# An MLP's first product moved to sevens with early-staged sums, and every engine in source order

## The chip, the cores and the metric

One core of a Trainium2 chip runs the kernel. The metric is the device time of one execution, in microseconds (us). TensorE (PE) multiplies, VectorE (DVE), ScalarE (ACT) and GpSimd (POOL) do the rest, and SyncE (SP) issues the transfers.

## The reference

A hybrid decoder layer on 1024 tokens of width 1024: a gated merge of dilated attention and an RWKV-7 recurrence, then a squared-ReLU MLP, then a gated embedding. The change lies in the MLP alone:

```python
f = rmsnorm(h, ffn_pre_norm[i])
f = jnp.square(jax.nn.relu(f @ w_ff_in[i])) @ w_ff_out[i]      # 1024 -> 4096 -> 1024
h = h + rmsnorm(f, ffn_post_norm[i])
```

## The kernel before

The kernel is written as generators that yield the time of each TensorE step. A planner (`Order`) walks them on a model clock: dense work in `sch.add`, chains of other work in `sch.spawn`. So the order of TensorE's instructions is the order in which the planner emits them (`manual_schedule` for PE holds throughout). SP keeps the order of the source in most of the MLP too. VectorE, ScalarE and GpSimd are placed by the compiler's scheduler between the end of the recurrence and the last part of the MLP; elsewhere `manual_schedule(engines=OTHERS)` puts them in source order as well.

Each float32 product is three matmuls (`mm3`): both operands are split into a high half (a ScalarE copy to fp32r) and a low half (a subtraction on VectorE or GpSimd), and high x high, high x low and low x high are accumulated in PSUM.

**First matrix.** Its 32 column blocks of 128 (`ff1`) are multiplied plainly: each block for two token halves of 512, over eight chunks of 128 of the width, 24 matmuls of 128x512 each time. `wload` fetches a block (`wr`) and splits it into `wh` and `wl`; `ff1_evac` applies ReLU and squares into `raw_h`. The normalised activations `f` come from `mixed(i)`, one chain for each of eight token tiles, whose end `put_T` transposes them (`tp`) and splits them. `ff1_first` starts on token half 0 while the tiles of half 1 are still made.

**Second matrix.** Two column blocks of the first matrix make a pair, which is 256 rows of the second. Fifteen of the sixteen pairs are multiplied in seven block products in place of eight (Winograd's form of Strassen): the pair's activations make four blocks (two of 128 rows x two token halves), and the weights four (two of 128 rows x two halves of 512 columns). `operands` builds the sums on GpSimd (`sum`, `ws`), `split2` splits them (`duo`), and `product` runs 4 x 3 matmuls per block product and adds each result from PSUM to `tot` on VectorE. `prep(n + 2)` is called at the start of product n. The seven products stand between the half blocks of the next pair's first matrix. The last pair is multiplied plainly in `ff2_last`.

**Beside it.** `part` splits the weights of the last stage once and stores both halves in DRAM (`gp`, `gpl`, `pkg`), one unit every three products. `e_weights` and `last_weights` load them for the stage after the MLP.

```python
MUL = (2, 1, 6, 5, 3, 7, 4)
INTO = {1: (0, 0), 6: (1, 0), 5: (1, 1), 3: (0, 1), 7: (1, 1), 4: (1, 0), 2: (0, 0)}
FIRST = (2, 1, 7)                     # products that open a new PSUM bank; the others add to the last one
```

Of the kernel before, what the change touches and what calls it, by code (L numbers as in the profile page):

```python
# [10 lines left out]
F32 = mybir.dt.float32  # L11
# [233 lines left out]
def layer(ctx: ExitStack, tc: tile.TileContext, x, pT, wz, wup, w_out, wff1, w_ff2, w_ple, w_pleg,  # L245
# [1067 lines left out]
    class Split:  # L1313
        def __init__(self, pcs):
            self.p = [k2(t) for t in pcs]

        def __getitem__(self, key):
            _, k, t = key
            return self.p[k // 2][:, k % 2, t]

# [43 lines left out]
    def out_1(i):  # L1364
        def body():
            h, ts = tok(i)
            if i == 0:
# [4 lines left out]
                pc = pieces(GA, "f0", F32R)  # L1372
                fT[0][0], fT[1][0] = Split(pc[0:4]), Split(pc[4:8])
# [7 lines left out]
    fT = [[None, None], [None, None]]  # L1381
# [9 lines left out]
    def put_T(srcs, hi, lo, i):  # L1391
        ts = slice(i * 128, i * 128 + 128)
        for b in range(2):
# [3 lines left out]
            if isinstance(hi, Split):  # L1397
                for q in range(2):
                    o = 2 * b + q
                    S.activation(hi.p[o][:, :, ts], ps[:, 2 * q:2 * q + 2, :], AF.Copy)  # L1400
                    V.tensor_tensor(lo.p[o][:, :, ts], ps[:, 2 * q:2 * q + 2, :], hi.p[o][:, :, ts],
                                    OP.subtract)
            else:
                o = (slice(None), slice(4 * b, 4 * b + 4), ts)
                S.activation(hi[o], ps, AF.Copy)
                V.tensor_tensor(lo[o], ps, hi[o], OP.subtract)
            sch.hold(tag)

    def mixed(i, ps):
        h = i // 4  # L1410
        yield from wait(lambda: i == 0 or ("M", i - 1) in done and (i < 2 or i - 2 in t_f))
        if i == 4:
            for p in range(2):
                fT[p][1] = mtile("hl"[p], 0, [128, KT, 512], f"f1{p}", F32R)
# [15 lines left out]
        yield from put_T(hh, fT[0][h], fT[1][h], i % 4)  # L1430
        t_f[i] = sch.dep + 0.1

# [10 lines left out]
    def totals():  # L1443
        for m in range(2):
            tot.append(mtile("hl"[m], 1, [128, 2, 4, 512], f"tot{m}", F32))

    def acc(i, c):
        return tot[i // 4][:, c, i % 4]

    def ff1_half(ps, hi, lo, h):  # L1450
        return mm3(ps, [(hi[:, k * 128:(k + 1) * 128], lo[:, k * 128:(k + 1) * 128],
                         fT[0][h][:, k, slice(0, 512)], fT[1][h][:, k, slice(0, 512)]) for k in range(KT)])

    def ff1_evac(ps, j, h):
        p, x = j // 2, 2 * (j % 2) + h
        if p not in raw_h:
            raw_h[p] = rtile([128, 4, 512], "hr", ("BK", "UV")[p % 2])
# [72 lines left out]
    def prep(n):  # L1530
        p, i = n // 7, MUL[n % 7]
        if p >= NP - 1:
            return
# [403 lines left out]
```

## Time and profile before

| what | value |
|---|---|
| time, median of 3 runs | 1776.96 us (1774.38 to 1780.42) |
| profiled execution: time, span | 1773.19 us, 1771.4 us |
| mean granted TensorE clock | 0.999 |
| busy share PE / DVE / ACT / POOL | 98% / 57% / 41% / 38% |
| MLP, first to last matmul of the fifteen pairs | 982.4 to 1626.1 us |
| DMA over the span | 175.51 MB, mean 99 GB/s |

The span runs from the first to the last instruction; the time has some 2 us more around it. A busy share counts pipelined matmuls by their length, so 98% says that TensorE hardly ever had nothing in flight, not that each matmul was at its best pace. In the tables of groups a line reads: source line, engine, operation, output and inputs, shapes, count, then busy time, mean ns of one, and the idle time ahead of it with what ended it.

### The profile page before, as it was taken

To read this page: it belongs to the slowest core of one execution; us is meant where nothing else is said; L and a number is where in the kernel's file an instruction comes from. 1 tells how busy PE (TensorE), PEld (TensorE's weight loads), DVE (VectorE), ACT (ScalarE), POOL (GpSimd) and SP (SyncE) were. 2 spreads that over 40 slices of the span, in tenths; PEclk is the share of its full clock that TensorE was granted. 3 is DMA by queue.
4 is the path that set the end of the run, shared out by engine and by line. 5 is a ranking of instruction groups with operands and counts; after the bars stand their busy time and mean duration, and the time that the engine had idled before them with its cause. 6 is when DMAs were issued, how large, how long until landed. Compare 5 with 4: busy or idle time off the path is not lost.

```text
span 1771.4 us, 25935 instructions
## 1 busy us (share of the span) xinstructions
PE 1743.8 (98%) x10192; PEld 1423.4 (80%) x10192; DVE 1017.1 (57%) x1834; ACT 732.3 (41%) x1315; POOL 670.5 (38%) x423
## 2 busy tenths in 40 slices
PE   9999989999999999999999999999999999999998
PEld 8787877878877777778888878888788888888887
DVE  6289777776534233353735466665666566556643
ACT  5824343432344343542434434343334334333454
POOL 1344131231232323332230266666665566652311
PEclk9999999999999999999999999999999999999999
DMA  4621121212332222333524132332232232305611
GB/s 163 211 95 37 49 78 47 98 43 96 86 134 84 60 60 72 110 111 135 201 96 139 64 113 95 94 115 87 92 118 91 84 95 90 123 9 179 214 48 48
DMA packets 67132, 175.51 MB, mean 99 GB/s; under 512 B 7745, under 2 KB 8129, under 8 KB 66498
## 3 DMA queue, kind: packets, MB, share of 16 engines
q1 hardware_dynamic: 67010, 173.86, 29.6%
q8 instruction: 80, 1.31, 0.3%
q14 instruction: 42, 0.34, 0.1%
HBM read 125.20 MB, written 41.94 MB: 94 GB/s over the span
## 4 chain that ended last, share of the span: by engine, by line
PE 82%; DVE 5%; DMA 5%; ACT 3%; POOL 2%; issue 2%; SPq 0%; DVEq 0%; ACTq 0%; POOLq 0%
PE z L294 18%; PE z L296 18%; PE z L292 18%; PE bk L292 6%; PE bk L294 5%; PE bk L296 5%; PE sc L275 1%; DVE xy L113 1%; PE y L275 1%; PE po L275 1%; PE pt L283 1%; PE A L275 1%; PE wr L275 1%; PE fq L275 1%; POOL wl L113 1%
## 5 line engine op out<-in xcount | busy, mean ns | idle before, releaser
L113 POOL TENSOR_TENSOR wl<-wr,wh 128x1024 fp32r<-128x1024 f32 (+1 forms) x87 | 208.0, 2392 | 431.4 <-ACT wh L113 412.2
L113 DVE TENSOR_TENSOR tot<-tot,bk 128x512 f32<-128x512 f32 x420 | 272.7, 682 | 129.9 <-PE bk L296 129.7
L292 PE MATMUL z<-uh,wh 128*128 128x512 f32 (+1 forms) x800 | 312.3, 390 | 5.5 <-ACT part L113 3.0
L296 PE MATMUL z<-uh,wl 128*128 128x512 f32 (+1 forms) x800 | 312.6, 391 | 2.7 <-POOL wl L113 2.7
L294 PE MATMUL z<-ul,wh 128*128 128x512 f32 (+1 forms) x800 | 313.6, 392 | 1.3 <-DVE ul L113 1.3
L292 PE MATMUL z<-f,wh 128*128 128x512 f32 x496 | 193.2, 389 | 0.3 <-ACT f L113 0.3
L294 PE MATMUL z<-f,wh 128*128 128x512 f32 x496 | 193.1, 389 | 0.2 <-DVE f L113 0.2
L296 PE MATMUL z<-f,wl 128*128 128x512 f32 x496 | 193.0, 389 | 0.0
L292 PEld LDWEIGHTS z<-uh,wh 128*128 128x128 f32 x800 | 151.1, 189 | 36.2 <-ACT part L113 3.5
L296 PEld LDWEIGHTS z<-uh,wl 128*128 128x128 f32 x800 | 151.0, 189 | 34.1 <-POOL wl L113 4.0
L294 PEld LDWEIGHTS z<-ul,wh 128*128 128x128 f32 x800 | 151.2, 189 | 32.3 <-issue 3.6
L292 PE MATMUL bk<-duo 128*128 128x512 f32 x420 | 164.3, 391 | 4.0 <-DVE tot L113 3.9
L294 PE MATMUL bk<-duo 128*128 128x512 f32 x420 | 163.5, 389 | 0.0
L296 PE MATMUL bk<-duo 128*128 128x512 f32 x420 | 163.5, 389 | 0.0
L113 ACT ACTIVATE wh<-wr 128x1024 fp32r<-128x1024 f32 (+1 forms) x87 | 90.3, 1038 | 119.0 <-PE z L294 89.8
L113 POOL TENSOR_TENSOR duo<-w2r,duo 128x512 fp32r<-128x512 f32 x45 | 66.7, 1483 | 166.0 <-ACT duo L113 166.0
L113 POOL TENSOR_TENSOR duo<-ws,duo 128x512 fp32r<-128x512 f32 x60 | 81.0, 1350 | 122.3 <-ACT duo L113 119.0
L292 PEld LDWEIGHTS z<-f,wh 128*128 128x128 f32 x496 | 93.1, 188 | 20.0 <-ACT f L113 0.5
L294 PEld LDWEIGHTS z<-f,wh 128*128 128x128 f32 x496 | 93.1, 188 | 19.8 <-DVE f L113 0.5
L296 PEld LDWEIGHTS z<-f,wl 128*128 128x128 f32 x496 | 93.1, 188 | 19.2
L292 PEld LDWEIGHTS bk<-duo 128*128 128x128 f32 x420 | 78.8, 188 | 23.7 <-DVE tot L113 7.0
L296 PEld LDWEIGHTS bk<-duo 128*128 128x128 f32 x420 | 78.8, 188 | 16.4
(312 smaller groups left out, 3203.5 us busy)
## 6 DMA issues: line engine op xcount, KB each, us to landing
wr<-in_wz_dram SPq DMA_DIRECT2D x48, 512.0 KB, 3.7
wr<-in_wff_dram SPq DMA_DIRECT2D x31, 512.0 KB, 3.6
w2r<-in_w_ff_dram SPq DMA_DIRECT2D x30, 512.0 KB, 4.2
xt<-in_x_dram SPq DMA_DIRECT2D x16, 512.0 KB, 4.3
gscr<-gst SPq DMA_DIRECT2D x32, 256.0 KB, 2.0
g<-gscr SPq DMA_DIRECT2D x16, 512.0 KB, 4.2
wpg<-pkg SPq DMA_DIRECT2D x16, 512.0 KB, 6.7
sw<-qk SPq DMA_DIRECT2D x48, 128.0 KB, 2.3
```

The lines of the kernel that those rows point to most:

```text
L113: return f(*a, **kw)
L275: PE.matmul(out_, a, b, start=start, stop=stop)
L283: PE.transpose(out_, a, ident if idn is None else idn)
L292: PE.matmul(ps, ah, bh, start=start and i == 0, stop=False, skip_group_check=not start)
L294: PE.matmul(ps, ah, bl, start=False, stop=False, skip_group_check=not start)
L296: PE.matmul(ps, al, bh, start=False, stop=i == n - 1, skip_group_check=not start)
```

## The change

The first matrix goes to sevens too. Its blocks are: the activations' two halves of the width (512 each) for two token halves, and for each pair of column blocks four quarters of the weights. `put_f` makes seven operand tiles F[1] to F[7] from the activations once (for token half 1, six more ScalarE copies and the sums and low halves on VectorE and GpSimd, per token tile). Products 1 and 2 of a pair need only token half 0. All 32 of them (`early`) run first, 27 of them before token half 1 is asked for; the first product is stored to DRAM (`p1_scr`), their sum is activated and stored (`c_scr`). `take(p)` loads them back for each pair, `first` runs the other five products (6, 5, 7, 3, 4), and VectorE adds them to the loaded blocks. GpSimd makes the weights' sums (`w1_sum`), each in the place of a quarter, which `w1_raw` reloads.

The second matrix is multiplied in sevens for every other pair (`seven`, pairs 0, 2, ... 14) and plainly for the seven between (`plain`). For the sevens, the sums of weights are made and split one round ahead (`w2_sums`), stored to DRAM (`bs_scr`) and loaded back as operands. `pend` holds low-half subtractions and some transfers back until the next `flush()`, one chunk of three matmuls or one block later. `part` runs in the plain rounds, four units each.

From the first pair's five products on, `manual_schedule(engines=OTHERS)` holds for VectorE, ScalarE, GpSimd and SP.

```diff
-        yield from put_T(hh, fT[0][h], fT[1][h], i % 4)
+        yield from put_f(hh, i)
...
+    def put_f(srcs, i):
...
+        t2, t4 = (rtile([128, 4, 128], n, tag) for n, tag in (("t2", "pg"), ("t4", "yc")))
+        V.tensor_tensor(t2, d, at(1, 0), OP.add)
+        V.tensor_tensor(t2, t2, at(1, 1), OP.add)
+        G.tensor_tensor(c, c, at(1, 0), OP.subtract)
+        G.tensor_tensor(c, c, at(1, 1), OP.subtract)
+        G.tensor_tensor(t4, at(2, 0), t2, OP.subtract)
+        G.tensor_tensor(t4, t4, at(2, 1), OP.add)
+        for n, x, eng in ((7, d, V), (6, t2, V), (5, c, G), (4, t4, G)):
+            S.activation(at(n, 0), x, AF.Copy)
+            eng.tensor_tensor(at(n, 1), x, at(n, 0), OP.subtract)
...
-    MUL = (2, 1, 6, 5, 3, 7, 4)
+    MUL = (1, 6, 5, 3, 7, 4, 2)
-    FIRST = (2, 1, 7)
+    FIRST = (1, 7, 2)
...
+    SEQ = (6, 5, 7, 3, 4)
...
+    def w1_split(j):
...
+        S.activation(w[:, 0], src, AF.Copy)
+        lo = lambda: (V if j < NA and j % 4 == 3 else G).tensor_tensor(w[:, 1], src, w[:, 0], OP.subtract)
+        lo() if j < NA else pend.append(lo)
+
+    def w1_sum(p, n):
...
+        if n == 1:
+            G.tensor_tensor(at("s1"), at(21), at(22), OP.add)
+        if n == 2:
+            G.tensor_tensor(at(21), at(11), at(21), OP.subtract)
+        if n == 3:
+            G.tensor_tensor(at(11), at("s1"), at(11), OP.subtract)
+        if n == 4:
+            G.tensor_tensor(at(12), at(12), at(11), OP.subtract)
...
+    def early(j):
+        k, p, i = prods[j]
+        if k != 25:
+            a_raw(min(k + 6, NE) if k != 26 else 31)
...
+        yield from w1_mm(j, ps, i == 1)
+        dst = A_["out"][:, k % (4 if k < NA else 2)]
+        if i == 1:
+            S.activation(dst, ps, AF.Copy)
+        else:
+            S.activation(dst, ps, AF.Relu)
+            S.activation(dst, dst, AF.Square)
+        SY.dma_start((p1_scr if i == 1 else c_scr)[p], dst)
...
+    def first(j):
+        k, p, i = prods[j]
+        n = SEQ.index(i)
+        if n == 3:
+            if p == 0:
+                w1_sum(1, 1)
+                w1_sum(1, 2)
+            w1_sum(p + 1, 3)
+        if p:
+            w1_split(j + 2)
+        late = p == 0
+        if n == 0 + late:
+            pend.append(lambda: w1_raw(p + 1, 21, 22, 11))
+        if n == 1 + late:
+            pend.append(lambda: w1_raw(p + 1, 12))
+        if n == 2 and p:
+            w1_sum(p + 1, 1)
+            w1_sum(p + 1, 2)
+        if n == 4:
+            w1_sum(p + 1, 4)
...
+        yield from w1_mm(j, ps, n < 2)
+        x = raw_h[p][:, {6: 1, 5: 3, 7: 3, 3: 1, 4: 2}[i]]
+        V.tensor_tensor(x, x, ps, OP.add)
+        if i in (7, 3, 4):
+            S.activation(x, x, AF.Relu)
+            S.activation(x, x, AF.Square)
...
+    def mlp():
+        last["turn"] = tc.manual_schedule(engines={mybir.EngineType.SP})
+        last["turn"].__enter__()
+        while sch.t < t_f.get(3, 1e9):
+            yield 0.0
+        for j in range(NA):
+            beside(j)
+            yield from early(j)
+        while sch.t < t_f.get(7, 1e9):
+            yield 0.0
+        last["turn"].__exit__(None, None, None)
+        last["turn"] = tc.manual_schedule(engines=OTHERS)
+        last["turn"].__enter__()
+        for n in range(5):
+            beside(NA + 2 * n)
+            yield from chunks(4 * n + 4)
+            beside(NA + 2 * n + 1)
+            Y["j"] += 1
+            yield from early(NA + 2 * n + 1)
+            flush()
+        prep(0)
+        prep(1)
+        flush()
+        for p in range(1, NP):
+            Y["n"] = 0
+            e = p - 1
+            if e % 2 == 0:
+                for x in range(7):
+                    yield from chunks((20 * x + 23) // 7 if p < NP - 1 else (3, 6, 9, 13, 17, 20, 20)[x])
+                    yield from seven(items.index((e, x)))
+                    if x == 0:
+                        load_w2(p)
+                    if x == 4:
+                        take(p + 1)
...
+                continue
+            for u in range(8):
+                yield from chunks((20 * u + 23) // 8)
+                if u == 0:
+                    load_w2(p)
+                yield from plain(items.index((e, u // 2)), u % 2)
+                if u == 1:
+                    take(p + 1)
+                    w2_sums(p, 0)
+                if 0 < u < 6:
+                    w2_sums(p, u)
+                part(2 * p - 4 + u // 2, u % 2)
...
     def split2(t, tag, eng):
         d = rtile([128, 2, 512], "duo", tag, F32R)
         S.activation(d[:, 0], t, AF.Copy)
-        eng.tensor_tensor(d[:, 1], t, d[:, 0], OP.subtract)
+        pend.append(lambda: eng.tensor_tensor(d[:, 1], t, d[:, 0], OP.subtract))
         return d
...
     def prep(n):
...
+        if e % 2 == 0:
+            i, room = MUL[x], rooms(e)[x % 3]
+            a = split2(operand(e, i), room[0], G)
+            if i in (2, 1, 3):
+                b = split2(w_blocks(e)[{2: 2, 1: 0, 3: 3}[i]], room[1], G)
+            else:
+                b = rtile([128, 2, 512], "duo", room[1], F32R)
+                SY.dma_start(b.bitcast(F32), bs_scr[e, i])
+            duo[n] = a, b
+            return
...
+    def plain(n, part):
+        e, x = items[n]
+        if part == 0:
+            prep(n + 2)
+        m, c = 1 - x // 2, x % 2
+        a, (hi, lo) = duo[e, m], ops["w"]
+        for t in (2 * part, 2 * part + 1):
+            ts = slice(t * 128, t * 128 + 128)
+            ps = bank(XB)
+            yield from mm3(ps, [(a[j][:, 0, ts], a[j][:, 1, ts], hi[:, j, halves[c]], lo[:, j, halves[c]])
+                                for j in range(2)])
+            V.tensor_tensor(tot[m][c][:, t], tot[m][c][:, t], ps, OP.add)
+            flush()
...
+    def part(u, x):
...
+            gp["t"] = rtile([128, 512], "gp", "gst")
+            SY.dma_start(gp["t"], src[:, c] if len(src.shape) == 2 else src[:, u % 2])
             return
+        raw, hi = gp["t"], rtile([128, 512], "gph", "gst", F32R)
+        lo = raw.bitcast(F32R)
         S.activation(hi, raw, AF.Copy)
         V.tensor_tensor(lo, raw, hi, OP.subtract)
         SY.dma_start(dst[:, k, 0, c], hi.bitcast(F32))
         SY.dma_start(dst[:, k, 1, c], lo.bitcast(F32))
...
-    ff1_first()
-    for j in range(2, 2 * NP):
-        ff1(j)
+    sch.add(mlp)
```

More of the change, by code (lines that the diff above doesn't have):

```diff
@@ L1444, in totals @@
         for m in range(2):
-            tot.append(mtile("hl"[m], 1, [128, 2, 4, 512], f"tot{m}", F32))
+            t = rtile([128, 2, 4, 512], "tot", GA[m])
+            tot.append([t[:, 0], t[:, 1]])
     def acc(i, c):
[L1448 to L1456, printed above, removed]
-            raw_h[p] = rtile([128, 4, 512], "hr", ("BK", "UV")[p % 2])
-        f1 = rtile([128, 512], "f1", "gst")
-        S.activation(f1, ps, AF.Relu)
-        S.activation(raw_h[p][:, x], f1, AF.Square)
-        if x == 3 and p == NP - 1:
-            last_split(1, (1,), ())
+        return tot[i // 4][c][:, i % 4]
@@ new lines, in w1_slot, with w1_raw @@
+    def w1_slot(p, n):
+        if n == 22:
+            return W1[22, p % 2]
+        if n == "s1" and p == 0:
+            if "s10" not in W1:
+                W1["s10"] = rtile([128, 512], "sum", "ex")
+            return W1["s10"]
+        return W1[n]
+    def w1_raw(p, *names):
+        for n in names:
+            if p < NP:
+                SY.dma_start(w1_slot(p, n), quarter(p, (11, 12, 21, 22).index(n)))
+    early_ = []
+    for p in range(0, NP, 2):
+        early_ += [(p, 1), (p + 1, 1), (p, 2), (p + 1, 2)]
@@ new lines, in layer, with chunks, take @@
+    Y = {"j": NA, "g": None, "n": 0}
+    def chunks(n):
+        while Y["n"] < n:
+            if Y["g"] is None:
+                Y["g"] = first(Y["j"])
+                Y["j"] += 1
+            for _ in range(3):
+                yield next(Y["g"])
+            flush()
+            Y["n"] += 1
+            if Y["n"] % 4 == 0:
+                for _ in Y["g"]:
+                    pass
+                Y["g"] = None
+    def take(p):
+        if p < NP:
+            raw_h[p] = rtile([128, 4, 512], "hr", ("BK", "UV")[p % 2])
+            for x, src in ((1, p1_scr), (3, p1_scr), (2, p1_scr), (0, c_scr)):
+                SY.dma_start(raw_h[p][:, x], src[p])
@@ L1464, in last_split, with mlp_ahead @@
+    def mlp_ahead(x):
+        if x == 0:
+            w1_tiles()
+            for k in range(4):
+                a_raw(k)
+        else:
+            for j in range(3):
+                w1_split(j)
+            a_raw(4)
+            a_raw(5)
     def last_split(k, hs, ws):
@@ L1538, in layer, with seven @@
+    XB = ("s1", "s2", "s3", "m0", "m1")
     chain = [None] * 4
-    def product(n):
-        p, i = n // 7, MUL[n % 7]
+    def seven(n):
+        p, x = items[n]
+        i = MUL[x]
         prep(n + 2)
@@ L1683, in last_weights @@
     def last_weights():
-        pg = pieces(GA, "wpg", F32R)
-        P["wpg"] = [[Split(pg[4 * p:4 * p + 4]), mtile("hl"[p], 0, [128, KT, 512], "wpg", F32R)]
-                    for p in range(2)]
+        P["wpg"] = [[mtile("hl"[p], 1 - c, [128, KT, 512], "wpg", F32R) for c in range(2)] for p in range(2)]
         P["g3"] = rtile([128, D], "g3", "v")
```

300 lines of the change are left out of this document (172 added, 128 removed).

## The prediction

> **What bounds the kernel now.** I read the page first: busy shares, clock, chain. Then I took windows over the MLP, its groups by line, its waits, and two pieces of the timeline.
>
> ```profile
> span 1771.4 us, 25935 instructions
> PE 1743.8 (98%) x10192; PEld 1423.4 (80%) x10192; DVE 1017.1 (57%) x1834; ACT 732.3 (41%) x1315; POOL 670.5 (38%) x423
> PEclk9999999999999999999999999999999999999999
> PE 82%; DVE 5%; DMA 5%; ACT 3%; POOL 2%; issue 2%; SPq 0%; DVEq 0%; ACTq 0%; POOLq 0%
> ```
> TensorE is busy nearly always, at full clock, and holds 82% of the chain. The time is a count of matmuls times a spacing, plus a few stalls. The MLP is z<-f (first matrix) and bk<-duo (second matrix):
>
> ```profile
> L292 PE MATMUL z<-f,wh 128*128 128x512 f32 x496 | 193.2, 389 | 0.3 <-ACT f L113 0.3
> L292 PE MATMUL z<-f,w 128*128 128x512 f32 x16 | 6.3, 395 | 0.0
> L292 PE MATMUL bk<-duo 128*128 128x512 f32 x420 | 164.3, 391 | 4.0 <-DVE tot L113 3.9
> L283 PE MATMUL tp<-cs,hh 128*128 128x128 f32 x24 | 3.1, 272 | 0.0
> ```
> Of z and bk each row stands for three (lines 292, 294, 296): (496 + 16) x 3 = 1536 matmuls for the first matrix and 420 x 3 = 1260 for the second, 2796 together. 389 ns is the pipelined length of one, not its price. The price is the spacing:
>
> ```profile
> 1402.12 0.39 PE L292 MATMUL z<-f,wh 128*128 128x512 f32 x1
> ...
> 1413.00 0.39 PE L292 MATMUL z<-f,wh 128*128 128x512 f32 x1
> ```
> Between these two starts lie four groups of twelve (half a z block, one product, twice): 10.88 / 48 = 0.2267 us each. At that, 2796 are 633.9 us. The windows (columns: PE, PEld, DVE, ACT, POOL busy, clock, DMA share, GB/s):
>
> ```profile
> 982.00:1010.00 28.00, 27.47 (x132) 22.55 (x131) 12.86 (x25) 14.11 (x30) 7.34 (x6) 1.00 0.09 34
> 1010.00:1050.00 40.00, 38.67 (x169) 31.00 (x168) 23.54 (x37) 13.80 (x24) 25.63 (x18) 1.00 0.30 105
> 1080.00:1240.00 160.00, 160.00 (x707) 132.34 (x706) 99.01 (x146) 62.12 (x102) 100.26 (x66) 1.00 0.29 93
> 982.00:1626.00 644.00, 639.49 (x2823) 526.83 (x2822) 389.10 (x579) 248.06 (x412) 381.02 (x253) 1.00 0.28 92
> ```
> The MLP fills 982.4 to 1626.1, 643.7 us. Beyond its 633.9 us lie 24 transposes (tp, under 3.1 us) and stalls of some 7 us: 644.00 - 639.49 = 4.5 us shown as TensorE idle, the rest restarts. In the steady stretch (third row) TensorE never idles, GpSimd is at 63% and VectorE at 62%. What TensorE waits for, and what the others wait for, in the MLP:
>
> ```profile
> PE bk L292 <- DVE tot L113: 3.9, 4, 1.7
> POOL duo L113 <- ACT duo L113: 235.7, 74, 34.4
> DVE tot L113 <- PE bk L296: 142.0, 58, 13.5
> ```
> The helpers wait for TensorE and each other; it hardly waits for them. One exception is worth seeing:
>
> ```profile
> 1241.35 0.63 ACT L113 ACTIVATE gp<-gp 128x512 fp32r<-128x512 f32 x1 [5.16 <-DMA gp<-in_w_pleg_dram]
> 1242.01 0.69 DVE L113 TENSOR_TENSOR gpl<-gp 128x512 fp32r<-128x512 f32 x1 [5.07 <-ACT gp L113]
> 1242.62 0.68 DVE L113 TENSOR_TENSOR tot<-tot,bk 128x512 f32<-128x512 f32 x1
> 1243.35 0.50 PE L292 MATMUL bk<-duo 128*128 128x512 f32 x1 [1.70 <-DVE tot L113]
> ```
> A late load blocked ScalarE, the subtraction behind it blocked VectorE, and the accumulation behind that cost TensorE 1.70 us. That is what an in-order engine does with one late operand.
>
> **The matmuls.** First matrix: a pair of 256 columns took 2 x 2 x 8 x 3 = 96 matmuls; in sevens it takes 7 x 4 x 3 = 84. Sixteen pairs: 1536 becomes 1344. Second matrix: fifteen pairs in sevens (84 each) become eight in sevens and seven plain (96): 1260 becomes 1344. Net -192 + 84 = -108, times 0.2267 = **-24.5 us**. All are 128x512, so the spacing holds. Up to 982 us the matmuls are the same, and behind 1626 us too (only tags move).
>
> **What helpers must do per pair.** From pair 1 on, a round has 60 matmuls of the first matrix (five products; two were staged early) and 84 or 96 of the second: 144 x 0.2267 = 32.6 us and 156 x 0.2267 = 35.4 us, where a round was 180 x 0.2267 = 40.8 us. Prices:
>
> ```profile
> L113 POOL TENSOR_TENSOR duo<-ws,duo 128x512 fp32r<-128x512 f32 x60 | 81.0, 1350 | 122.3 <-ACT duo L113 119.0
> L113 POOL TENSOR_TENSOR duo<-w2r,duo 128x512 fp32r<-128x512 f32 x45 | 66.7, 1483 | 166.0 <-ACT duo L113 166.0
> L113 POOL TENSOR_TENSOR ws<-w2r 128x512 f32<-128x512 f32 x30 | 47.0, 1569 | 11.2 <-PE tp L283 5.5 <-DMA w2r<-in_w_ff_dram 3.0 <-PE bk L296 0.8
> L113 DVE TENSOR_TENSOR tot<-tot,bk 128x512 f32<-128x512 f32 x420 | 272.7, 682 | 129.9 <-PE bk L296 129.7
> L113 DVE TENSOR_TENSOR duo<-hr,duo 128x512 fp32r<-128x512 f32 x45 | 40.6, 901 | 0.4 <-ACT duo L113 0.4
> L113 ACT ACTIVATE hr<-f 128x512 f32<-128x512 f32 x64 | 40.4, 632 | 1.9
> L113 ACT ACTIVATE f<-z 128x512 f32<-128x512 f32 x64 | 37.5, 586 | 35.1 <-PE z L296 35.0
> ```
> GpSimd, round with sevens: 5 low halves and 4 sums for the first matrix, 7 low halves for the second, 4 for the plain pair that follows: 20. Plain round: 5 + 4, 3 for the next sevens, 4 sums and 4 low halves staged to DRAM: 20. At 1.40 (between 1.35 and 1.57, nearer the larger group) that is 28.0 us, 86% and 79%. VectorE: with sevens 28 + 5 accumulations at 0.682 and 4 others at 0.90, 26.1 us (80%); plain 16 + 5 and 8 others, 21.5 us (61%). ScalarE: 24 copies or squares at 0.63 in either, 15 us. All fit under TensorE, so no engine becomes the bound by its work alone.
>
> **Order.** In order, an engine that is 86% full has to be fed in time. A second-matrix operand is prepared at the start of product n for product n + 2: two products of 12 x 0.2267 = 2.72 us and two runs of 20 / 7 chunks (0.68 us, three matmuls) of the first matrix, 9.3 us. GpSimd's largest burst is 4 operations a product (5.6 us against 4.6 us of TensorE), so it falls 1 to 2 us behind and recovers: cost 0, cover 9 us. An accumulation chain is rewritten one product later, 4 us of cover for 0.68 us of VectorE. ScalarE waits once per pair for GpSimd's sum before a weight copy (1.4 us), needed 13 us later. SP's reload of a quarter waits for GpSimd's subtraction of its old content; behind it on SP stands the load of a staged operand, with those 9.3 us of lead.
>
> Staging adds DMA: quarters read again 8.4 MB, first products written 8.4 and read 16.8, second-matrix sums written 16.8 and read 16.8, 67 MB on 59 now (92 GB/s x 644 us). 126 MB in about 620 us are 204 GB/s, a share near 0.6. Landing times:
>
> ```profile
> w2r<-in_w_ff_dram SPq DMA_DIRECT2D x28, 512.0 KB, 4.0
> gp<-in_w_pleg_dram SPq DMA_DIRECT2D x16, 256.0 KB, 2.7
> pkg<-gpl SPq DMA_DIRECT2D x16, 256.0 KB, 4.8
> L132 SPq DMA_DIRECT2D pkg<-gp x16: 326/425/474, 1242.0 to 1507.6; - x16
> wpg<-pkg SPq DMA_DIRECT2D x5, 512.0 KB, 8.1
> ```
> The last row is of the crowded end of the MLP. At 4.0 us a staged load is well inside its 9.3 us; at 8.1 us, with one subtraction of 1.4 us ahead of it on SP, it is 0.2 us late, 6 us over the 32 staged loads. I take 0, as three of the four rows are far under the lead, and keep 6 as the bound.
>
> **Where I expect new stalls.** (a) 982 to 1010: ten early products ask ScalarE for 1.53 us each (a copy 0.63, an evacuation of 0.59 or 0.59 + 0.63, on average 0.90), four token tiles for six copies (14.4 us), two norm chains of three squares and small steps for some 6: 36 us in 28. The tiles aren't needed until product 27, 73 us on, so 0 if products go first, 8 if not; 3 taken, nearer 0, because the first window shows ScalarE half idle and TensorE losing 0.53. (b) First pair: 120 matmuls, 27.2 us, for 19 GpSimd operations, 26.6 us. Then the first second-matrix product stands nine matmuls (2.0 us) behind its preparation: evacuation 1.2, two copies 1.3, two subtractions 2.8, 5.3 us. Bounds 0 and 8; 4 taken, a little over 5.3 - 2.0. (c) The four units of gate-weight staging in each plain round. One buffer makes load, copy, subtraction, store a loop: 2.7 + 0.6 + 0.7 + 4.8 + two issues of 0.4 = 9.6 us, where 35.4 / 4 = 8.8 us stand between one load and the next (three products, 3 x 40.8 / 7 = 17.5 us, before). It slips 0.8 us a unit, 2.4 us by the last, behind which VectorE's accumulations stand as at 1242.01; five banks cover about 4. Bounds 0 and 4 a round; 0.7 taken, 5 in seven rounds. (d) Elsewhere 1 (bounds 0 and 6, by the staged loads). Sum 13, against 7 that go with the old code: +6.
>
> **Sum.** 1773.19 (the profiled execution; span 1771.4) - 24.5 + 6 = 1754.7, a gain of 18.5. That execution is 3.8 us under the median of the runs, 1776.96, so the forecast is **1758 us**, 1.0% faster.
>
> **A rule of the Trainium skill.** The longest against the median duration (min/median/max) tells what slows what:
>
> ```profile
> L113 POOL TENSOR_TENSOR duo<-ws,duo x60: 1279/1295/1807, 1005.0 to 1608.5; 128x512 fp32r<-128x512 f32 x60
> L113 DVE TENSOR_TENSOR tot<-tot,bk x420: 671/681/689, 1023.3 to 1663.5; 128x512 f32<-128x512 f32 x140
> L113 DVE TENSOR_TENSOR duo<-hr,duo x45: 674/692/1712, 992.0 to 1607.9; 128x512 fp32r<-128x512 f32 x45
> ```
> The accumulation, which reads one operand from PSUM, never stretches; subtractions with both operands in SBUF do, by up to 1.0 us, and GpSimd's by 0.5. A round now has 4 to 8 such VectorE operations where it had about 9. The Trainium skill, SBUF — State Buffer, section "SBUF: two separate sides", says that VectorE and GpSimd share a port pair under an exclusive lock, and that a VectorE operation takes it only in a two-port mode or with two SBUF inputs. It would speak against filling both engines to 80%. By that rule and these rows, GpSimd would need 20 x 1.29 + 4 x 0.69 = 28.6 us with sevens and 31.3 us plain: still under TensorE, the sum unchanged. The trace agrees.
>
> **Rivals.** (1) Given back in waits: every round loses 1.6 us in waits of the kind at 1241.35 to 1243.35, 15 x 1.6 = 24, while some 5 of the old 7 go: 1777 - 24.5 + 24 - 5, about **1772**. For it: four engines in strict order and twice the DMA. Against: a lead of 9.3 us where that stall had none. (2) Slower: GpSimd keeps waiting for ScalarE's copies. It waited 235.7 us in the MLP, 15.7 a pair; if w us a round stay, a round lasts 28.0 + w, and the loss is 8 (28.0 + w - 32.6) + 7 (28.0 + w - 35.4) = 15 w - 88.6. From w = 7.5 it eats the whole 24.5; at w = 8.5, about half of today's, 39 is lost: 1776.96 - 24.5 + 39 - 7 = **1784**. For it: ScalarE itself now stands in order behind late evacuations. Against: most of those 235.7 us are idleness for want of work, and subtractions are issued a chunk behind their copies. (3) No new stalls, and the old 7 us gone: 1777 - 24.5 - 5 = **1747**. (4) The change doesn't do what it says: fewer than 108 matmuls saved; the source excludes that.
>
> **Chances.** Forecast with gains of 10 to 24 us (1753 to 1767): 0.60. No stalls: 0.08. Given back: 0.16, of which 0.10 within 0.3% (5.3 us, about what a measurement tells from no change) and 0.06 faster. GpSimd-bound: 0.16. So faster 0.74, same 0.10, slower 0.16. The range, 1745 to 1785, takes in the no-stall case and rival 2 at its price; what lies beyond is some 0.05 below and 0.10 above. The upper ends of (a) to (d) together, 8 + 8 + 28 + 6 - 7 - 24.5 = +18.5, would reach 1795, which I leave out as four ends at once.
>
> **What would show it.** In the trace after: 2688 matmuls of 0.2267 spacing in an MLP of about 625 us; GpSimd near 82% in the rounds; TensorE idle near the first early products, behind the first pair and late in plain rounds, each by a few us. GpSimd idle under 4 us a round refutes rival 2, TensorE idle over 20 us in the MLP refutes the sum, and a bs load landing after its product's start would show the DMA bound that I priced at nothing.

## The result, and the profile after

| what | before | after |
|---|---|---|
| time, median of the runs | 1777.09 us (1774.38 to 1780.42) | 1840.64 us (1836.35 to 1844.69) |
| profiled execution: time, span | 1773.19 us, 1771.4 us | 1837.83 us, 1836.0 us |
| mean granted TensorE clock | 0.999 | 0.983 |
| data moved | 175.51 MB | 242.66 MB |

The changed kernel is slower: a ratio of 1.0356, with a 95% interval of 1.0323 to 1.039. The forecast was 1758 us, 0.989 of the time before. On the page of the kernel after, the matmuls are indeed fewer (10084, which is 10192 - 108), but TensorE's share of the chain of waits has fallen from 82% to 63%:

```profile
span 1836.0 us, 26373 instructions
...
PE 1753.1 (95%) x10084; PEld 1417.0 (77%) x10084; DVE 1051.2 (57%) x1799; ACT 751.6 (41%) x1377; POOL 776.8 (42%) x532
...
PE 63%; DVE 10%; DMA 8%; POOL 8%; ACT 5%; issue 4%; SPq 1%; POOLq 0%; DVEq 0%; ACTq 0%
```

Two windows of the same kernel, one over the early products and one over the MLP (columns as in the prediction: PE, PEld, DVE, ACT, POOL busy, clock, DMA share, GB/s):

```profile
990.00:1060.00 70.00, 54.40 (x217) 42.16 (x216) 39.26 (x40) 36.43 (x73) 53.18 (x36) 0.90 0.38 128
...
990.00:1690.00 700.00, 643.51 (x2714) 516.33 (x2712) 418.19 (x549) 272.11 (x486) 492.22 (x363) 0.97 0.51 181
```

TensorE, which lost 0.53 us in the first 28 us of this stage before, is idle for 70.00 - 54.40 = 15.6 us in the first window, and for 700.00 - 643.51 = 56.5 us in all of the second. The granted clock, 1.00 in every window of before, is 0.90 and 0.97.

The waits of the changed kernel over the MLP (total, times, longest). The first row is VectorE's, the others are TensorE's five largest:

```profile
DVE gp L113 <- ACT gph L113: 92.3, 25, 8.3
...
PE bk L292 <- DMA duo<-bs: 16.9, 7, 3.6
PE bk L292 <- DVE tot L113: 15.9, 8, 2.6
PE bk L292 <- ACT pa L113: 15.6, 7, 5.5
PE z L296 <- POOL wl L113: 1.8, 1, 1.8
PE bk L294 <- POOL duo L113: 1.6, 1, 1.6
```

Three causes of much the same size. The timeline has one case of each (start, length, engine, operation, idle time ahead and its releaser):

```profile
997.64 0.63 ACT L113 ACTIVATE f<-t 128x512 fp32r<-128x512 f32 x1 [2.75 <-POOL t L113]
...
1000.43 0.59 ACT L113 ACTIVATE pa<-bk 128x512 f32<-128x512 f32 x1
...
1001.07 0.79 PE L292 MATMUL bk<-f,wl 128*128 128x512 f32 x1 [5.48 <-ACT pa L113]
...
1001.66 0.63 PE L294 MATMUL bk<-f,wl 128*128 128x512 f32 x1
...
1002.65 1.72 POOL L113 TENSOR_TENSOR wh<-wa,wh 128x512 fp32r<-128x512 f32 x1
...
1003.16 1.76 DVE L113 TENSOR_TENSOR t<-d,f 128x512 f32<-128x512 f32 x1
...
1004.34 1.72 POOL L113 TENSOR_TENSOR c<-c,f 128x512 f32<-128x512 f32 x1
...
1004.85 1.76 DVE L113 TENSOR_TENSOR f<-d,f 128x512 fp32r<-128x512 f32 x1
...
1006.09 0.63 ACT L113 ACTIVATE f<-c 128x512 fp32r<-128x512 f32 x1 [3.03 <-POOL c L113]
...
1187.27 0.63 ACT L113 ACTIVATE wl<-wr 128x512 fp32r<-128x512 f32 x1 [2.85 <-POOL wr L113]
...
1188.33 0.62 ACT L113 ACTIVATE gph<-gp 128x512 fp32r<-128x512 f32 x1
...
1188.98 1.32 DVE L113 TENSOR_TENSOR gp<-gp,gph 128x512 fp32r<-128x512 f32 x1 [5.06 <-ACT gph L113]
...
1193.29 1.66 DVE L113 TENSOR_TENSOR sum<-sum,hr 128x512 f32<-128x512 f32 x1
...
1194.87 1.27 DVE L113 TENSOR_TENSOR tot<-tot,bk 128x512 f32<-128x512 f32 x2
...
1195.60 0.50 PE L292 MATMUL bk<-duo 128*128 128x512 f32 x1 [1.35 <-DVE tot L113]
...
1421.81 0.33 SPq L132 DMA_DIRECT2D gp<-in_w_pleg_dram  x1
...
1422.50 0.50 PE L292 MATMUL bk<-duo 128*128 128x512 f32 x1 [2.30 <-DVE tot L113]
...
1425.99 0.32 SPq L132 DMA_DIRECT2D pkg<-gph  x1
...
1426.57 1.29 POOL L113 TENSOR_TENSOR wh<-wr,wh 128x512 fp32r<-128x512 f32 x1 [2.63 <-ACT wh L113]
...
1426.72 0.32 SPq L132 DMA_DIRECT2D pkg<-gp  x1
...
1427.88 1.28 SPq L132 DMA_DIRECT2D wr<-in_wff_dram  x3
...
1429.21 0.43 SPq L132 DMA_DIRECT2D duo<-bs  x1
...
1432.96 0.39 PE L296 MATMUL z<-f,wh 128*128 128x512 f32 x1
...
1435.64 0.47 PE L292 MATMUL bk<-duo 128*128 128x512 f32 x1 [2.29 <-DMA duo<-bs]
```

First stretch, the early products. GpSimd and VectorE take turns: 1002.65, 1004.34 on the one, 1003.16, 1004.85 on the other, each 1.7 us long, where VectorE's subtraction took 0.69 (median) in the kernel before. ScalarE stands in its queue at copies whose sums GpSimd has not made (2.75 us at 997.64, 3.03 at 1006.09), and the evacuation of a bank (`pa`, 1000.43) stands behind them: for that TensorE waited 5.48 us. Once started, a matmul lasts 0.63 us in place of 0.39.

Second stretch, a plain round. ScalarE waits for GpSimd's `wr`, so the copy `gph` of the staged gate weights is late; VectorE stands 5.06 us at its subtraction, does two slow sums, and reaches the accumulation (`tot`) at 1194.87. TensorE waited 1.35 us for it.

Third stretch, the start of a round with sevens. The first product starts at 1422.50, and the staged operand for 1433.2 should be asked for there. SyncE issues it at 1429.21, because two things stand ahead of it. The two stores of the last staging unit (`pkg`) wait for ScalarE's copy and VectorE's subtraction of weights whose load was issued only at 1421.81; they go out at 1425.99 and 1426.72. Behind them the reload of three quarters (`wr`, 1427.88) waits for GpSimd's subtraction, which ended at 1426.57 + 1.29 = 1427.86, and its three issues take another 1.28 us. The staged load then takes 6.3 us to land, behind the reload's transfers. The last matmul before the operand starts at 1432.96, and the next one 2.68 us later. The two stores stand there in six of the seven rounds in which TensorE waited for a staged operand.

To sum such losses up, I took the distance between the starts of neighbouring 128x512 matmuls from 930 us on, less 0.2267 us each. An excess of more than 0.28 us in one distance is "gap"; smaller ones are "half pace" (the short restart behind every wait is among them).

| from 930 us on | gap | half pace | largest gaps by what they waited for |
|---|---|---|---|
| before | 5.5 us | 3.0 us | tot 5.0 |
| after | 65.1 us | 25.4 us | staged operand 18.0, tot 17.7, pa 16.7 |

The account closes: -24.5 (108 matmuls) + 59.6 (gaps) + 22.4 (half pace) + 6.6 (the end of the stage ahead of the MLP, 988.8 against 982.2 us) = +64.1; the spans differ by 1836.0 - 1771.4 = 64.6 us. Of the 6.6 us, 5.1 are not the change's, as the kernel with holes shows below.

### The profile page after: what moved, and what is told of

Read it like the earlier page. It is cut to its first block, busy times and chain, and to the rows that moved or that the text cites. A ratio compares the mean times of both kernels' runs of the same rounds, so it can differ in the third digit from the quotient of the medians.

```text
span 1836.0 us, 26373 instructions
## 1 busy us (share of the span) xinstructions
PE 1753.1 (95%) x10084; PEld 1417.0 (77%) x10084; DVE 1051.2 (57%) x1799; ACT 751.6 (41%) x1377; POOL 776.8 (42%) x532
## 2 busy tenths in 40 slices
DMA packets 99392, 242.66 MB, mean 132 GB/s; under 512 B 11329, under 2 KB 11713, under 8 KB 98754
## 3 DMA queue, kind: packets, MB, share of 16 engines
q8 instruction: 79, 1.29, 0.3%
## 4 chain that ended last, share of the span: by engine, by line
PE 63%; DVE 10%; DMA 8%; POOL 8%; ACT 5%; issue 4%; SPq 1%; POOLq 0%; DVEq 0%; ACTq 0%
PE z L294 13%; PE z L296 13%; PE z L292 13%; PE bk L292 4%; PE bk L294 4%; PE bk L296 4%; DMA duo<-bs 2%; DVE tot L113 2%; DMA hr<-cscr 2%; POOL duo L113 2%; SPq L132 1%; POOL wh L113 1%; POOL wl L113 1%; PE sc L275 1%; DVE g L113 1%
## 5 line engine op out<-in xcount | busy, mean ns | idle before, releaser
L113 POOL TENSOR_TENSOR wl<-wr,wh 128x1024 fp32r<-128x1024 f32 (+1 forms) x56 | 133.0, 2375 | 420.9 <-ACT wh L113 401.7
L113 DVE TENSOR_TENSOR tot<-tot,bk 128x512 f32<-128x512 f32 x336 | 217.5, 680 | 52.6 <-PE bk L296 52.4
L292 PE MATMUL bk<-duo 128*128 128x512 f32 x224 | 94.9, 424 | 33.1 <-DMA duo<-bs 16.9
L113 ACT ACTIVATE wh<-wr 128x1024 fp32r<-128x1024 f32 (+2 forms) x94 | 81.0, 861 | 100.9 <-PE z L294 55.9
L113 ACT ACTIVATE hr<-hr 128x512 f32<-128x512 f32 x96 | 60.7, 632 | 134.0 <-DVE hr L113 132.5
L113 POOL TENSOR_TENSOR duo<-sum,duo 128x512 fp32r<-128x512 f32 x64 | 89.0, 1395 | 25.6 <-ACT duo L113 24.9
L113 DVE TENSOR_TENSOR gp<-gp,gph 128x512 fp32r<-128x512 f32 x28 | 32.9, 1175 | 115.8 <-ACT gph L113 92.3
L294 PE MATMUL bk<-duo 128*128 128x512 f32 x224 | 91.8, 410 | 1.6 <-POOL duo L113 1.6
L296 PE MATMUL bk<-duo 128*128 128x512 f32 x224 | 91.6, 409 | 0.0
L292 PE MATMUL bk<-ws,duo 128*128 128x512 f32 x224 | 87.1, 389 | 0.0
L294 PE MATMUL bk<-ws,duo 128*128 128x512 f32 x224 | 87.1, 389 | 0.0
L296 PE MATMUL bk<-ws,duo 128*128 128x512 f32 x224 | 87.1, 389 | 0.0
L292 PEld LDWEIGHTS bk<-duo 128*128 128x128 f32 x224 | 44.2, 197 | 55.6 <-DVE tot L113 25.0
L113 DVE TENSOR_TENSOR hr<-hr,z 128x512 f32<-128x512 f32 x80 | 54.3, 679 | 51.0 <-PE z L296 29.2
L292 PE MATMUL z<-f,wh 128*128 128x512 f32 x212 | 83.1, 392 | 0.0
```

The lines of the kernel that those rows point to most:

```text
L113: return f(*a, **kw)
L292: PE.matmul(ps, ah, bh, start=start and i == 0, stop=False, skip_group_check=not start)
L294: PE.matmul(ps, ah, bl, start=False, stop=False, skip_group_check=not start)
L296: PE.matmul(ps, al, bh, start=False, stop=i == n - 1, skip_group_check=not start)
```

## The experiments

The kernel before took 1779.65 us beside the first four kernels and 1775.94 beside the next four. One execution lies within some 5 us of its kernel's median, so single times are read together with their gaps and half pace. One to five each alter one thing in the changed kernel.

**1. The staging units spread over all rounds**, two in each, in place of four in each plain round (the first hunk is in the rounds with sevens):

```diff
+    if x in (0, 2, 3, 5):
+        part(2 * p - 2 + x // 3, (0, 2, 3, 5).index(x) % 2)
...
-    part(2 * p - 4 + u // 2, u % 2)
+    if u in (0, 3, 4, 7):
+        part(2 * p - 2 + u // 4, (0, 3, 4, 7).index(u) % 2)
```

> The changed kernel with the 28 gate-weight staging units (load, ScalarE copy, VectorE subtraction, two stores) spread two to a round over all rounds, in place of four in each plain round. Theory A (a unit that is not ready blocks VectorE, and SP behind it): the TensorE gaps behind VectorE's accumulations (17.7 us) and behind the staged operands (18.0 us) mostly go, and with them about half of the 25 us at half pace: near 1795 us. Rival B (the units are only the place where a general lag of the ordered engines shows): the gaps move to other operations, 1825 to 1838 us.

1816.20 us; gaps 50.0, half pace 18.3. Its waits:

```profile
DVE gp L113 <- ACT gph L113: 13.8, 14, 2.3
...
PE bk L292 <- DVE tot L113: 4.4, 4, 2.2
```

VectorE's wait for the copy `gph` went from 92.3 to 13.8 us, and TensorE's for `tot` from 15.9 to 4.4. The loop of four units in a plain round is the cause of that third of the loss. The time expected, 1795 us, was missed: the waits for staged operands, which theory A had going too, stayed at 14.0 of 16.9 us.

**2. No source order for VectorE, ScalarE and GpSimd in the rounds** (SyncE alone keeps it):

```diff
-        last["turn"].__exit__(None, None, None)
-        last["turn"] = tc.manual_schedule(engines=OTHERS)
-        last["turn"].__enter__()
```

> The changed kernel, but VectorE, ScalarE and GpSimd placed by the compiler's scheduler in the rounds too, as in the kernel before; only SP stays in source order. Rival B (strict order couples the engines): the gaps in the rounds, 36 us and some 15 us of half pace, mostly go: near 1790 us. Theory A (the units block wherever they stand) or the shared-port theory (GpSimd and VectorE slow each other whatever the order): 1820 us or more, perhaps slower than the changed kernel, since no order was chosen with the staging in mind.

1839.96 us, gaps 72.0, half pace 22.6:

```profile
PE bk L292 <- DVE tot L113: 24.2, 17, 4.4
PE bk L292 <- ACT pa L113: 20.6, 6, 5.2
```

The staged operands come in time here (0.4 us lost in all), but the accumulation is later, 24.2 us. On balance nothing: another order of the three engines moves the losses and does not lower their sum.

**3. Source order already from the first early product:**

```diff
-        last["turn"] = tc.manual_schedule(engines={mybir.EngineType.SP})
+        last["turn"] = tc.manual_schedule(engines=OTHERS)
...
-        last["turn"].__exit__(None, None, None)
-        last["turn"] = tc.manual_schedule(engines=OTHERS)
-        last["turn"].__enter__()
```

> The changed kernel with source order for all four engines from the first early product on, not only from the first pair's five products. If the scheduler's placing of ScalarE's waits caused the gaps between 989 and 1060 us (16.7 us behind evacuations, some 6 us half pace), they shrink by at least half: 1826 us or less. If the operand tiles for token half 1 need more of GpSimd and VectorE than there is, source order blocks in the same places: 1835 us or more.

1855.01 us, gaps 80.5, half pace 24.2; one gap of 19.4 us for a late evacuation:

```profile
PE bk L292 <- ACT pa L113: 30.6, 3, 19.4
```

In order, each evacuation stands behind the token tile's work, and that is late. It is the tiles' work itself that has to become lighter:

**4. The sums and low halves of the second token half on VectorE, not GpSimd:**

```diff
-        G.tensor_tensor(c, c, at(1, 0), OP.subtract)
+        V.tensor_tensor(c, c, at(1, 0), OP.subtract)
...
-        for n, x, eng in ((7, d, V), (6, t2, V), (5, c, G), (4, t4, G)):
+        for n, x, eng in ((7, d, V), (6, t2, V), (5, c, V), (4, t4, V)):
```

> The changed kernel with the sums and low halves of F[4] and F[5] (six operations per token tile) on VectorE in place of GpSimd. Shared-port theory (in 989 to 1035 us each VectorE operation of 0.7 us takes 1.7 us because it waits for a GpSimd one, and the other way round): the operations fall to 0.7 us, ScalarE no longer waits for GpSimd there, the evacuation gaps fall from 16.7 to under 6 us: near 1822 us. Rival (SP, held until 1014 us by the stores of the last hidden states, starves the loads and the stores of the early products): no change within 5 us.

1823.30 us, gaps 55.6, half pace 21.3. VectorE now does six more operations for each of four tiles. In the stretch below eight in a row have their short length again, while GpSimd stands idle (1000.3 to 1016.9); once it works again, three of VectorE's last 1.8 us each (1017.35 to 1023.17). TensorE's waits for evacuations fall from 15.6 to 6.9 us, of which one of 6.0 is left:

```profile
1002.61 0.68 DVE L113 TENSOR_TENSOR t<-f,t 128x512 f32<-128x512 f32 x1
...
1003.21 0.68 DVE L113 TENSOR_TENSOR f<-d,f 128x512 fp32r<-128x512 f32 x1
```

```profile
PE bk L292 <- ACT pa L113: 6.9, 2, 6.0
```

The edit takes the alternation away and shortens GpSimd's queue at once, so what each is worth is not shown apart. SyncE's row shows what is behind the wait that is left: four stores of `h` occupy its queue until 1009.29, waiting for VectorE, and the stores of first products, which free the evacuation's buffers, stand behind them.

```profile
994.70 14.59 SPq L132 DMA_DIRECT2D hscr<-hh  x4
```

**5. The reload of the quarters moved behind the first product of a round with sevens**, so behind the staged operand's load on SyncE:

```diff
-        if n == 0 + late:
+        if n == 0 + late and p % 2 == 0:
             pend.append(lambda: w1_raw(p + 1, 21, 22, 11))
...
                     if x == 0:
+                        w1_raw(p + 1, 21, 22, 11)
                         load_w2(p)
```

> One move alone: in rounds with sevens the reload of three first-matrix quarters (which waits on SyncE for GpSimd's subtraction) is issued behind the round's first product, so that the load of the staged operand no longer stands behind it. Theory (SyncE's order makes that load late): the 18.0 us that TensorE waits for staged operands fall under 4, the half-pace matmuls behind those waits lose 4 to 8 us, the profiled time goes from 1838 to about 1817 (1808 to 1824). Rival (the load is late because the transfers are crowded): issue moves earlier but landing takes as much longer, the waits stay near 18 us, and the time stays at 1838 within 4. Second rival (the quarter now comes late and GpSimd's sums wait): new waits of TensorE for GpSimd or ScalarE of 10 us or more, 1830 or above.

1815.26 us (1809.81 and 1820.70), a ratio to before of 1.0217 (1.0174 to 1.0261); gaps 48.2, half pace 14.7. In the timeline the load (`duo<-bs`) is now ahead of the reload:

```profile
1415.13 0.41 SPq L132 DMA_DIRECT2D duo<-bs  x1
...
1415.89 1.28 SPq L132 DMA_DIRECT2D wr<-in_wff_dram  x3
```

TensorE waits for a staged operand nowhere. Over all 32 staged loads the median time from issue to landing (the last number) stayed the same, in the changed kernel and then in this one:

```profile
duo<-bs SPq DMA_DIRECT2D x32, 512.0 KB, 4.1
```

```profile
duo<-bs SPq DMA_DIRECT2D x32, 512.0 KB, 4.3
```

The load that TensorE had waited for, the second of a round, gained twice, on average over the second to the seventh round: it is issued 2.4 us earlier, counted from the round's first load, and lands in 4.4 us in place of 5.7, as the reload's transfers are no longer ahead of it. The third load of a round takes 5.2 to 8.5 us here, and TensorE does not wait for it. So the loss was the load's place in SyncE's order, not the bandwidth. The two stores of the staging unit still stand ahead: at 1415.13 the load is 4.7 us behind the start of the round's first product (1410.40).

**6. Edits 1, 4 and 5 together**, and in the last round the loads of the last weights ahead of another load:

```diff
+                        if x == 5:
+                            last_split(0, (0, 1), (0,))
+                            last_split(1, (1, 0), (1,))
                         if x in (1, 2, 5):
                             e_weights((1, 2, 5).index(x))
-                        if x == 5:
-                            last_split(0, (0, 1), (0,))
-                            last_split(1, (1, 0), (1,))
```

> Four edits together: staging units two a round over all rounds; the sums and low halves of the second token half on VectorE; the reload of the quarters behind the first product of a seven round; the last weights' loads ahead of another load in the last round. Theory (four separate causes whose costs add): 1838 less 21 (units), 15 (sums), 20 (staged loads) and 5 (last weights) = 1777, range 1766 to 1792, TensorE's gaps from 930 us on near 20 us and half pace near 6. Rival (the waits only move on, as each engine is too full in order): 1800 or more with gaps over 40.

1777.70 us, beside 1775.94 for the kernel before: 1.0005 (0.9992 to 1.0018). Gaps 19.5, half pace 9.0. The separate causes add: one by one their edits gained 24.4, 17.3 and 25.4 us (67.1 together), all in one 62.9. Two of the largest waits that are left:

```profile
PE bk L292 <- ACT pa L113: 5.8, 2, 5.5
PE bk L294 <- DMA lwl<-pkl: 2.3, 2, 1.3
```

**7. The stores of `h` on ScalarE's queue** in the kernel with four edits:

```diff
-            SY.dma_start(h_scr[i][:, halves[c]], hh[c])
         r = ss2(hh, [xt[:, halves[0]], xt[:, halves[1]]])
+        for c in range(2):
+            nc.scalar.dma_start(h_scr[i][:, halves[c]], hh[c])
```

> The four edits, and the stores of the residual h issued by ScalarE's queue behind its two squares, not by SyncE, where they hold back the early weights' loads and the stores of first products. Theory: the wait of about 6 us for an evacuated buffer near 1013 goes, with about 2 us of half pace: 8 us under the kernel with the four edits, about 1769 (1758 to 1782). Rival (the issues cost ScalarE as much as they free on SyncE): the same as with four edits, within 3 us.

1778.44 us, 1.0010 (0.9994 to 1.0026). The gap of 5.7 us at 1012 is gone and one of 2.6 stands at 1027, with small ones at 1008, 1021 and 1071 (0.4, 0.5 and 1.0 us); the stage ahead, in which the first of these issues fall, starts 1.4 us later than with four edits and ends 4.0 us later, so 2.6 us are lost in it. The rival holds: the loss moved.

**8. Holes in the kernel before.** What is the half pace? ScalarE holds TensorE up at thirty places, by one to ten copies of a PSUM bank into the next:

```diff
+                if t == 0 and i in (1, 7):
+                    hole[0] += 1
+                    for _ in range((hole[0] - 1) % 10 + 1):
+                        S.activation(chain[t], old, AF.Copy)
```

> The kernel before, with thirty holes in TensorE's work in the second matrix: ahead of the products 1 and 7 of each pair ScalarE copies the finished PSUM bank into the next one, once to ten times over (extra work whose result is overwritten, the output is unchanged). Theory (the half pace in the changed kernel is the clock's answer to an idle TensorE): holes up to some 1.6 us cost their own length; behind many of those of 2.2 us and more eight to ten matmuls run at 0.43 us in place of 0.2267, 1.5 to 2.0 us extra; in the thirty together 15 to 40 us of half pace, on some 80 to 110 us of gaps. Rival (the half pace comes from the changed kernel's own operands, loads or ports): no run of 0.43 us spacing behind any hole, half pace under 5 us as in the kernel before.

1970.05 us, gaps 154.7, half pace 43.1 (both above what was expected, as the holes came out longer), in a kernel whose operands, loads and split of work are those of before. A short hole and a long one in its timeline:

```profile
1299.97 0.50 PE L292 MATMUL bk<-duo 128*128 128x512 f32 x1 [1.66 <-ACT bk L113]
...
1300.31 0.39 PE L294 MATMUL bk<-duo 128*128 128x512 f32 x1
...
1428.41 0.80 PE L292 MATMUL bk<-duo 128*128 128x512 f32 x1 [4.97 <-ACT bk L113]
...
1429.01 0.63 PE L294 MATMUL bk<-duo 128*128 128x512 f32 x1
...
1429.43 0.63 PE L296 MATMUL bk<-duo 128*128 128x512 f32 x1
```

Behind 1.66 us of idleness the next matmul follows after 0.34 us, and then one each 0.23. Behind 4.97 us they come 0.43 us apart until 1431.14. The windows say why (the granted clock is the third number from the end):

```profile
1428.40:1431.10 2.70, 2.69 (x6) 2.16 (x7) 0.88 (x2) 0.00 (x0) 0.00 (x0) 0.50 0.00 0
1431.20:1434.00 2.80, 2.80 (x14) 2.29 (x13) 2.60 (x4) 1.15 (x2) 0.00 (x0) 0.99 0.00 0
```

Of five gaps of 1.7 to 2.7 us none was followed by such a run; of 24 of 3.0 us and more, 23 were, by 6 to 14 matmuls, 1.4 to 3.0 us extra each, however long the hole. The Trainium skill, TensorE: Matmul & The Clock Gate, "Part 1: The HAM clock gate", gives this mechanism: after an idle window of some 3.4 us on a free-running counter the array's clock is halved, until it has been busy for about as long. The clock in this trace agrees in its steps: it is 0.5 in stretches of 3.41 us or two or three times that, on one fixed grid (here from 1427.82 to 1431.23). A whole step of idleness is not needed, though. In this kernel and in the changed one, every step at full clock with 1.90 us or more of idle TensorE was followed by a halved one, and none with 1.79 us or less. So it matters how a gap lies on the grid: the hole of 3.3 us that cost only its length lay across two steps, 1.72 and 1.40 us. In the changed kernel 9 of 13 gaps of 2.2 us and more were followed by half pace, and one of 2.14 us too. The kernel before, with at most 1.70 us idle in a step of the MLP, was not halved there at all.

The same trace settles the 6.6 us ahead of the MLP. Here are the last rows of that stage in the kernel before, in the changed one and in this one, which to that point has the code of the kernel before:

```profile
L296 PE MATMUL z<-wo,mt x128: 387/389/479, 891.2 to 982.2; 128*128 128x512 f32 x128
```

```profile
L296 PE MATMUL z<-wo,mt x128: 387/389/498, 896.3 to 988.8; 128*128 128x512 f32 x128
```

```profile
L296 PE MATMUL z<-wo,mt x128: 388/389/479, 898.2 to 989.1; 128*128 128x512 f32 x128
```

The unaltered code starts this stage even later, at 898.2, so the profiled execution of before was an early one. The lead is old: near 500 us, in matmuls that are the same in all three, the changed kernel is 5.4 us behind it and this one 7.7. The stage itself lasts 91.0 us before, 92.5 in the changed kernel and 90.9 here; those 1.5 us arise where `put_f` already works, and belong to the change.

**9. Two more edits, without and with a third,** on the kernel with four. In the first pair VectorE makes the low halves of the weights and of the first two second-matrix operands; in the last round one load and one subtraction swap their buffers; and a `flush()` stands between `prep(0)` and `prep(1)`. The third edit gives the scaled activations of tiles 4 to 7 a buffer of their own, stores `h` behind the tile's work, and starts tiles 5 to 7 later.

```diff
-        lo = lambda: (V if j < NA and j % 4 == 3 else G).tensor_tensor(...)
+        lo = lambda: (V if (j % 4 == 3 if j < NA else j < NA + 10) else G).tensor_tensor(...)
...
         prep(0)
+        flush()
         prep(1)
...
-            last[k] = (rtile([128, 2, 512], "lhl", ("Ep", "En")[k], F32R),
-                       rtile([128, 1024], "lwl", ("kk", "MP")[k], F32R))
+            last[k] = (rtile([128, 2, 512], "lhl", ("kk", "En")[k], F32R),
+                       rtile([128, 1024], "lwl", ("Ep", "MP")[k], F32R))
...
-            a = split2(operand(e, i), room[0], G)
+            eng = V if n < 2 else G
+            a = split2(operand(e, i), room[0], eng)
```

Without the third:

> The same without the edit of the stores of h. Theory: the 9 us at 1012 stay, the rest goes: 1768 (1760 to 1775). Rival: no better than with four edits, 1777 within 3.

1769.00 us beside 1776.95: 0.9952 (0.9933 to 0.9972). Gaps 12.4, half pace 7.3. The theory held. With the third:

```diff
-        yield from wait(lambda: i == 0 or ("M", i - 1) in done and (i < 2 or i - 2 in t_f))
+        yield from wait(lambda: i == 0 or ("M", i - 1) in done and (i < 2 or i - 2 in t_f) and (i < 5 or i - 1 in t_f))
...
+        to = [hs[:, c] for c in range(2)]
...
-            V.scalar_tensor_tensor(hh[c], hh[c], r, gn["f"][:, halves[c]], op0=OP.mult, op1=OP.mult)
+            V.scalar_tensor_tensor(to[c], hh[c], r, gn["f"][:, halves[c]], op0=OP.mult, op1=OP.mult)
...
+        yield from put_f(to, i)
+        for c in range(2):
+            SY.dma_start(h_scr[i][:, halves[c]], hh[c])
```

> The four edits, and three more: in the first pair the low halves of its weights and of its first two second-matrix operands are made by VectorE, not GpSimd; in the last round the two loads and subtractions that share buffers swap them, so that no load waits for the last product but one; from token tile 4 on the scaled activations get a buffer of their own, and the stores of h stand on SyncE behind the tile's work, not ahead of it. Theory: what the kernel with four edits (1777.7) still loses is 5.7 us and 3 of half pace at 1012, 6 us and 2 at 1068 to 1108, and 3.5 and 1.5 at the end; most of it goes, 1760 (1752 to 1770), so under the kernel before (1776) by 0.3 to 1.3%. Rival (the losses move on to the next late operand, as with the stores on ScalarE's queue): 1772 to 1780.

1771.42 us, 0.9969 (0.9953 to 0.9986). (The load of `x` for tile 7, issued at 975.9, overwrites tile 5's buffer before tile 5 reads it at 980.5, so tile 5's `h` has another `x` in it; the instructions are those described.) The 5.7 us at 1011 shrank to 1.8, and 3.7 at 1037 and 2.8 at 1072 came in their place. The losses moved on, as the rival has it; the time lies between the two ranges.

**10. The first eight stores and eight weight loads of the early products on ScalarE's queue**, in the kernel with six edits:

```diff
-            SY.dma_start(A_["raw"][:, k % 4], quarter(p, i - 1))
+            (SY if k < 6 or k >= 14 else nc.scalar).dma_start(A_["raw"][:, k % 4], quarter(p, i - 1))
...
-        SY.dma_start((p1_scr if i == 1 else c_scr)[p], dst)
+        (SY if j >= 8 else nc.scalar).dma_start((p1_scr if i == 1 else c_scr)[p], dst)
```

> The six edits (four edits, first pair's low halves on VectorE, the last round's buffers swapped), and the stores of the first eight early products and the loads of early weights 6 to 13 issued by ScalarE's queue, where nothing waits for the late stores of h. Theory (SyncE's held queue alone makes the wait of 5.7 us at 1011): that wait and its 2.5 us of half pace go, 1769 less 8 = 1761 (1757 to 1766). Rival (ScalarE and VectorE are themselves too late there, so the wait moves to the next buffer or weight): 1766 to 1775, with a new wait of 3 us or more between 1005 and 1075.

1764.36 us beside 1777.56: 0.9938 (0.9919 to 0.9957): of all versions, the lowest ratio. The time is in the theory's range, but the wait at 1011 is still there, 4.0 us of it, as the rival has it, and the profiled spans without and with this edit are equal (1762.5 and 1762.0). The two intervals overlap, so what this edit itself is worth stays open.

## Why the prediction was wrong

**The matmuls: right.** 108 fewer at 0.2267 us. With gaps of 10.9 and half pace of 7.2, the span of the last kernel (experiment 10) comes to -24.5 + 5.4 + 4.2 + 5.9 (its later start, 988.1 against 982.2) = -9.0 against before, and 1762.0 - 1771.4 is -9.4. Of the 24.5 us, 13.2 show in the medians there (1777.56 - 1764.36), with most of what stood in the way gone.

**"All fit under TensorE, so no engine becomes the bound by its work alone": right, and not enough.** No engine was full. Rival 2, a round as long as GpSimd's work and its waits for ScalarE, was not the way it became slower: experiments 1 and 5 leave GpSimd's work in the rounds as it is, and each takes away one of the losses; TensorE's waits for GpSimd itself were 1.8, 1.6 and 0.8 us. The sign named for refuting it did not come, though: GpSimd, busy about 54 us in each 75 (two rounds), was idle for some 10 us a round, not under 4, and waits between GpSimd and ScalarE are links of all three chains above. The sign for a wrong sum did come: TensorE idle for 56.5 us, where 20 was the limit. The mechanism was that of rival 1 (given back in waits), priced at 24 us, where gaps and half pace cost 82.

**Order, "cover 9 us", cost 0: the step that failed first.** The 9.3 us run from the call of `prep` to the product, and I took them for the load's lead. On SyncE the load is issued only when all ahead of it have been: at 1429.21 it had 4.0 us left, and it took 6.3. I named the reload that waits for GpSimd, added one subtraction of 1.4 us and stopped there. That wait was the small part, 0.8 us. What I left out is the rest of the queue: the two stores of the staging unit ahead of the reload hold SyncE until 1427.04, 4.5 us behind the first product's start; the reload's own issues take 1.3 us; and behind its transfers the load lands in 6.3 us, where the median is 4.1. Cost: 18.0 us of gaps. What the prediction offered as the sign of a DMA bound, a staged load that lands late, was SyncE's order, as experiment 5 shows.

**(c), the staging loop: right in kind, 5 us taken, bound 28.** 17.7 us of gaps for `tot` in the changed kernel, 5.0 with the units spread. The loop of 9.6 us against 8.8 was the right place. What I left out is that its copy stands in ScalarE's order behind copies that wait for GpSimd, as in the second stretch above, which shifts the whole unit.

**(a), the early products: 3 us taken, bound 8; it was 16.7.** I counted ScalarE's work between 982 and 1010. The waits for `pa` lie between 1001 and 1055, and ScalarE was not full there (36.43 us busy of 70.00). It waited for GpSimd and VectorE, which held each other up.

**The rule on the shared port: right, and used wrongly.** The Trainium skill, SBUF — State Buffer, "SBUF: two separate sides", says that the loser of the lock blocks for the whole instruction. I added the locked times to a sum over a round and found them to fit. But the early products are not a round: in the first window above GpSimd is busy for 53.18 us of the 70 and VectorE for 39.26, stretched operations included, and a result comes late by the other engine's operation, after 1.76 us in place of 0.68. Experiment 4 takes the alternation away and most of these waits with it; GpSimd's shorter queue may have a part in that.

**(b), the first pair: right.** 4 us taken; the waits for GpSimd's `wl` and `duo` there are 3.4 us.

**The half pace: missing.** 22.4 us more of it than before, a quarter of the 82, follows from the gaps. The prediction priced each stall by its length alone; in the changed kernel most stalls of over 2.2 us cost about another 2, at half the clock.

## What to carry over

A lead counts from the issue, not from the call: for a load in an ordered queue, list what each instruction ahead of it waits for, and place the load ahead of anything that waits for a busy engine. Price a stall of TensorE of over some 2 us at its length and, where it can fall into one step of the clock, 2 us more, and break up a bundle of side work in some rounds before its loop is as long as the time between them. When several late operands cost the same, take them away one by one: here the costs added, and the change became a gain, about half of what its matmuls promise, only when nearly all were gone.

## What was not expected of the hardware

- Operations on VectorE and GpSimd with both operands in SBUF did not just stretch now and then: they alternated for 8 us at a time, 0.69 becoming 1.76 and 1.29 becoming 1.72 us.
- The half pace has a threshold in the idleness of TensorE within one 3.41 us step of the clock (in these two kernels none with 1.79 us, always with 1.90), and then a price that hardly depends on the gap: 1.4 to 3.0 us extra behind holes of 3.0 to 8.6 us.
- Twice the data in flight (195 GB/s in experiment 5 from 990 to 1690 us, against 92 over the MLP before) cost TensorE no wait for a staged operand once SyncE's order was mended, at a median of 4.3 us from issue to landing.
